# Where weight splits, two weight sums and a group of operand loads stand in the instruction order of a transformer-like layer

## The chip, the cores and the metric

The kernel runs on one core of a Trainium2 chip. The metric is the device time of one execution in microseconds (us); less is better. The median of three runs of the kernel before is 2864.06 us (2863.84 to 2871.59).

## The reference

One layer over 2048 tokens of width 1024, all in float32:

```python
xn = rms_norm(x, mix_norm_g)
aq, ak, av, mq, mk, mv, mo, i, f, ga, gm = split(xn @ w_in)
att = chunk_band_attention(aq, ak, av, rel_bias)      # chunks of 64, own and 8 previous
mq, mk = silu(causal_conv(mq)), silu(causal_conv(mk))
hm = mlstm_chunkwise(mq, mk, mv, i + b_i, f + b_f)    # matrix memory, a recurrence over chunks
m = sigmoid(mo) * headwise_rms_norm(hm)
y = sigmoid(ga) * (att @ w_att_proj) + sigmoid(gm) * (m @ w_mlstm_proj)
x = x + y @ w_out
x = x + square(relu(rms_norm(x) @ w_up)) @ w_down
return rms_norm(x, final_norm_g)
```

## The kernel before, in words

**Precision.** Every large product is made of three matmuls. A float32 operand is split into a rounded high part and the rest: ScalarE casts the high part (L435 for weights, L1032 and L1034 for activations), VectorE subtracts it from the operand (L437, L1037, L1039). A product is high by high, high by low and low by high (`mm3`, L496 to L498, and inline in the quads at L579 and L607).

**Weights.** A weight tile is 128 by 1024. It is loaded into one of four raw buffers (`wraw`) and split into one of three buffers (`wsplit`, two parts each); 459 tiles are split in this way, in the order in which `weights` lists them. `split_w` loads a tile and splits it; `quad_w` does so for the seven tiles of a quad out of four loaded ones. A raw buffer goes back to its pool with `late=LATE`, 3000 ns, and a split buffer goes back without, when the last matmul that reads it has been issued (the `fl.put(self.wsplit, w)` in `feature_tile`, `token_tiles`, `pair_tile`, `quad`, `quad_tok` and `down`).

**Quads.** Large products are computed on blocks of two by two with seven products in place of eight (Strassen's scheme in Winograd's form). A quad is seven weight tiles, m = 0 to 6, each multiplied with one of seven operands, and needs sums of weight blocks: `sum_w(q)` computes four of them for weight q, in two halves. For each half it takes four `ctx` tiles at once, loads four blocks (L399), does four subtractions on VectorE (L404) and stores their results to the DRAM tensor `wsum` (L1937); the second subtraction waits for the first store. The loader waits for these sums before it loads them (L417). Where the sums are made as the quad runs, `quad_w` does it on the raw tiles (L454). A quad's products share three PSUM places; `combine` adds them up with ScalarE copies (L1678) and VectorE adds (L1686), and a place is filled again only after its copy or add.

**Order.** Each engine runs its instructions in the order in which the program issues them. This order is written by a planner, `Flow`: each piece of work is a Python generator that yields waits, requests for buffers, and steps on an engine with an estimated length. The planner always issues the step that can start first by its own clock; among equal ones it goes by a priority, in which 0 (the splits) is before 1 (evacuations), 2 and 3 (the sums). `put(pool, item, late=...)` gives a buffer back at the planner's present time plus `late`; whoever takes it can't start before that by the planner's clock. `late` puts no wait into the program; it only moves the taker's instructions back in the order. Real waits are the semaphores between engines, which follow from the data and the buffers.

**Stages** (`dense`, priority 5, issues the main matmuls). The sequence has four blocks of 512 tokens. Block 0 and block 1 have their own input projections; beside them run the attention (L1196, L1227, L1258, L1263, L1208) and the recurrence (L1483 to L1556) of the block before. Then come, as pairs of weights, the projections of block 0 (`proj`); the quads of the gates ga0, ga1, gm0, gm1 for blocks 0 and 1; the projection of block 1 and the two quads of `w_out`; eleven quads of `w_in` for blocks 2 and 3, two of which (`quad_tok`, L607, for the values) have fourteen tiles with twelve matmuls each, where the others have 24 matmuls a tile; eight quads of `w_up` and the products with `w_down`; and the same from the projections on for blocks 2 and 3, whose attention and recurrence run beside the first `w_down`.

**The two sums.** Weights q = 2 and 3 are the quads of `w_out`. Their `sum_w` is spawned at the end of block 0's input projections, so it runs beside block 1. The other sums are spawned at the beginning of quads of `w_in` and `w_up`.

**The stored projection and the output operands.** `project_span(s)` projects block 2s+1 with `project`, whose results stay in eight `ctx` tiles (`y3`, set at L864 together with the event `yp_ev[2s+1]`). `take_rest`, one for each k from 0 to 3, takes three more `ctx` tiles, loads two tiles of the other block's projection into them (L1603), and makes from them and two of the eight kept ones the operands 2 to 6 of the w_out quad (adds at L1616, splits at L1034 and L1039). `load` in `after_out` takes eight `ctx` tiles, one after the other, and loads the residual input x into them (L1885), from the middle of the projection on (the event `go`). The quad's products are added to these (L1898). The pool `ctx` has sixteen tiles.

Of the kernel before, what the change touches and what calls it, by code (L numbers as in the profile page):

```python
# [45 lines left out]
N_G, N_O, N_F = 2, 2, 8  # L46
# [4 lines left out]
GATES = ("ga0", "ga1", "gm0", "gm1")  # L51
# [171 lines left out]


class Layer:
    LATE = 3000.0

    def __init__(self, tc, pool, psum, io):
        self.tc, self.nc, self.io = tc, tc.nc, io
# [95 lines left out]
    def weights(self):  # L325
# [12 lines left out]
        for name in GATES:  # L338
            yield quad(name)
# [75 lines left out]
    def split_w(self, i, src, raw, sent=None):  # L415
# [4 lines left out]
        yield from self.split_now(i, raw)  # L420
        self.fl.put(self.wraw, raw, late=self.LATE)

# [18 lines left out]
    def quad_w(self, i, q, kept, raws, evs):  # L441
# [33 lines left out]
        yield from sub(2, b, d, b)  # L475
        fl.put(self.wraw, d, late=self.LATE)
        yield "wait", [spilt[1]]
        yield from sub(3, a, c, a)
        fl.put(self.wraw, c, late=self.LATE)
        yield from self.split_now(i + 5, b)  # L480
        yield "wait", [spilt[2]]
        fl.put(self.wraw, b, late=self.LATE)
        yield from self.split_now(i + 6, a)
        yield "wait", [spilt[3]]
        fl.put(self.wraw, a, late=self.LATE)

# [13 lines left out]
    def feature_tile(self, srcs, evs, parts=1):  # L500

        fl = self.fl
        w = yield from self.next_w()
        wv = w.rearrange("p a (k c) -> p a k c", k=KT)
        got = []
        n = KT // parts
        for k in range(KT):
            if k % n == 0:
                got += (yield "dense", self.banks, 1)
            if evs[k] is not None:  # L510
                yield "wait", [evs[k]]
            yield "pe", 681
            self.mm3(got[-1], wv[:, 0, k], wv[:, 1, k], srcs[k][:, 0], srcs[k][:, 1],
                     k % n == 0, k % n == n - 1)
        fl.put(self.wsplit, w)
        return got

    def token_tiles(self, srcs, evs, after):

        fl = self.fl  # L520
        bank = [None] * NT
        nw = len(srcs) // 2
        for i in range(nw):
            w = yield from self.next_w()
            wv = w.rearrange("p a (k c) -> p a k c", k=2)
            for t in range(NT):
                if i == 0:
                    (bank[t],) = yield "dense", self.banks, 1
                for k in range(2):
                    g = 2 * i + k  # L530
                    if evs[g] is not None:
                        yield "wait", [evs[g]]
                    yield "pe", 681
                    a = srcs[g][:, :, t * P:(t + 1) * P]
                    self.mm3(bank[t], a[:, 0], a[:, 1], wv[:, 0, k], wv[:, 1, k],
                             g == 0, g == 2 * nw - 1)
                if i == nw - 1:
                    fl.spawn(after(t, bank[t]), 1)
            fl.put(self.wsplit, w)

    def pair_tile(self, srcs, evs, kind="dense"):

        fl = self.fl
        w = yield from self.next_w()
        wv = w.rearrange("p a (k n c) -> p a k n c", k=4, n=2)
        got = []
        for n in range(2):
            got += (yield kind, self.banks, 1)
            for k in range(4):
                if evs[k] is not None:  # L550
                    yield "wait", [evs[k]]
                yield "pe", 681
                self.mm3(got[-1], wv[:, 0, k, n], wv[:, 1, k, n], srcs[k][:, 0], srcs[k][:, 1], k == 0, k == 3)
        fl.put(self.wsplit, w)
        return got

    def quad(self, A, aev, after, release):


        fl = self.fl  # L560
        bank, clear = {}, {}
        mm = self.nc.tensor.matmul
        for m, z in enumerate(PLACES):
            w = yield from self.next_w()
            wv = w.rearrange("p a (k n c) -> p a k n c", k=4, n=2)
            for n in range(2):
                new = (z, n) not in bank
                if new:
                    (bank[z, n],) = yield "get", self.banks, 1
                else:  # L570
                    yield "wait", [clear[z, n]]
                ps = bank[z, n]
                for k in range(4):
                    if aev[m][k] is not None:
                        yield "wait", [aev[m][k]]
                    yield "pe", 681
                    a = A[m][k]
                    for x, y in ((0, 0), (0, 1), (1, 0)):
                        mm(ps, wv[:, x, k, n], a[:, y], start=new and k == 0 and x == y == 0,  # L579
                           stop=k == 3 and x == 1, skip_group_check=True)  # L580
                clear[z, n] = after(m, n, ps)
            fl.put(self.wsplit, w)
            if release:
                fl.put(self.rpool, *A[m])

    def quad_tok(self, p, A, aev, after):

        fl = self.fl
        bank, clear = {}, {}
        mm = self.nc.tensor.matmul  # L590
        for m, z in enumerate(PLACES):
            for kk in range(2):
                w = yield from self.next_w()
                wv = w.rearrange("p a (k c) -> p a k c", k=2)
                for n in range(2):
                    new = kk == 0 and (z, n) not in bank
                    if new:
                        (bank[z, n],) = yield "get", self.banks, 1
                    elif kk == 0:
                        yield "wait", [clear[z, n]]  # L600
                    ps = bank[z, n]
                    for k in range(2):
                        yield "wait", [aev[m][2 * kk + k]]
                        yield "pe", 681
                        a = A[m][2 * kk + k][:, :, (2 * p + n) * P:(2 * p + n + 1) * P]
                        for x, y in ((0, 0), (1, 0), (0, 1)):
                            mm(ps, a[:, y], wv[:, x, k], start=new and k == 0 and x == y == 0,  # L607
                               stop=kk == k == 1 and y == 1, skip_group_check=True)
                fl.put(self.wsplit, w)
            for n in range(2):  # L610
                clear[z, n] = after(m, n, bank[z, n])

    def down(self, s, m, ring, A, aev):

        fl = self.fl
        mm = self.nc.tensor.matmul
        bank = {}
        for c in range(4):
            for q in range(2):
                w = yield from self.next_w()  # L620
                wv = w.rearrange("p a (k n c) -> p a k n c", k=4, n=2)
                for n in range(2):
                    j = 2 * q + n
                    if c == 0:
                        (bank[j],) = yield "dense", self.banks, 1
                    for k in range(4):
                        yield "wait", [aev[m, c][k]]
                        yield "pe", 681
                        a = A[m, c, k]
                        self.mm3(bank[j], wv[:, 0, k, n], wv[:, 1, k, n], a[:, 0], a[:, 1],  # L630
                                 c == 0 and k == 0, c == 3 and k == 3)
                    if c == 3:
                        fl.spawn(self.add_down(s, m, j, bank[j]), 1)
                fl.put(self.wsplit, w)
            fl.put(ring, *[A[m, c, k] for k in range(4)])

    def dense(self):
        fl = self.fl
        none = [None] * KT
        for b in range(2):  # L640
# [40 lines left out]
                fl.spawn(self.evac_og(b, j, bk), 1)  # L681
            fl.put(self.rpool, *xs)
            fl.set(B["xs_free"])
            for q in range(N_G, N_G + N_O if b == 0 else 0):
                fl.spawn(self.sum_w(q), 3)
        for k in range(4):
            fl.spawn(self.take_rest(k, *G, self.xnd[:2], self.xn_kept[:2], 1.0), 2)

# [7 lines left out]
        fl.put(self.rpool, *self.blk[0]["mix"])  # L696
        self.banks.want = 0
        X, U = self.operands(), self.operands()
        for name in GATES:
            last = name == GATES[-1]  # L700
            if last:
                fl.spawn(self.take_mix(1), 1)
            yield from self.quad(*G, self.after_in(name, 0), release=last)
# [1161 lines left out]
    def after_out(self, s, q, U, go=None):  # L1865

        fl, nc = self.fl, self.nc
# [8 lines left out]
        def load():  # L1876
            if go is not None:
                yield "wait", [go]
            for w in ("a11", "a22", "a12", "a21"):
                for n in range(2):  # L1880
                    hi, h = where[w]
                    (x,) = yield "get", self.ctx, 1
                    xt[n][w] = x
                    yield "sp", 900, 2000
                    nc.sync.dma_start(x[:, :512], self.io["xt"][2 * s + h, 4 * hi + 2 * q + n])  # L1885
                    fl.set(ev[n][w])
# [454 lines left out]
```

## Time and profile before

| | us |
|---|---|
| median of three runs | 2864.06 |
| profiled execution | 2863.24 |
| its span | 2861.4 |
| TensorE matmuls busy | 2802.6 |
| VectorE busy | 2016.3 |
| ScalarE busy | 1529.6 |

Mean granted TensorE clock over the span is 0.997 of full speed. PE is TensorE, DVE VectorE, ACT ScalarE, SP or SPq SyncE, whose queue issues all the DMAs of data. A row of the groups reads: line, engine, operation, output and inputs, count, busy time and mean ns of one, and the idle time of the engine in front of it with what ended it. A row of the waits reads: who waited for whom, us in total, times, and the longest. In the order of time a row reads: start, duration, engine, line, operation, and in brackets the idle time before it and its releaser. Times of rows are counted from the span's start.

### The profile page before, as it was taken

The numbers are of one execution on the slowest core, as the hardware profiler recorded it, in microseconds if no ns is written. First come the engines' busy times: TensorE is split into PE (matmuls) and PEld (weight loads), VectorE is DVE, ScalarE is ACT, GpSimd is POOL, SyncE is SP. The second block draws the span as 40 slices with busy tenths as digits, with TensorE's granted clock in tenths as the row PEclk, the third lists the DMA queues.
The fourth block names the chain that finished last, engine by engine and source line by source line (L and its number), as shares of the span: only waits on it lengthen the run. The fifth ranks groups of instructions, "written<-read, shape, count | busy, mean of one in ns | idle before, by whom it ended". The sixth has DMA issues, their size and how long they took to land.

```text
span 2861.4 us, 39400 instructions
## 1 busy us (share of the span) xinstructions
PE 2802.6 (98%) x13528; PEld 2337.2 (82%) x13528; DVE 2016.3 (70%) x3745; ACT 1529.6 (53%) x2639; POOL 48.1 (2%) x100
## 2 busy tenths in 40 slices
PE   8999999999999999999999999999999999999998
PEld 7887888888878887878887888888887888888887
DVE  6795698657896866886667778789568744455565
ACT  5563467544354544575556566665435655554444
POOL 0010001000000000000000000000000000000000
PEclk9999999999999999999999999999999999999999
DMA  7878867648755687588877987876587655576563
GB/s 261 270 222 282 251 187 235 219 143 295 231 200 200 208 271 241 193 273 307 282 271 253 285 235 221 254 218 218 196 306 238 210 199 195 187 243 213 185 225 135
DMA packets 317736, 662.41 MB, mean 231 GB/s; under 512 B 35552, under 2 KB 62304, under 8 KB 317536
## 3 DMA queue, kind: packets, MB, share of 16 engines
q1 hardware_dynamic: 317536, 659.90, 70.3%
q8 instruction: 106, 1.74, 0.3%
q14 instruction: 94, 0.77, 0.1%
HBM read 462.63 MB, written 197.13 MB: 231 GB/s over the span
## 4 chain that ended last, share of the span: by engine, by line
PE 72%; DVE 13%; DMA 9%; ACT 3%; issue 2%; SPq 1%; POOL 0%; POOLq 0%; DVEq 0%; ACTq 0%
PE bank L579 32%; PE bank L496 10%; PE bank L497 10%; PE bank L498 10%; DVE wsp L437 3%; PE bank L607 2%; PE bank L1196 2%; DMA wsum<-ctx 2%; DVE r L1037 2%; DMA r<-u 1%; PE bank L1258 1%; PE bank L1227 1%; ACT wsp L435 1%; DVE sc L1233 1%; DMA ctx<-in_wf 1%
## 5 line engine op out<-in xcount | busy, mean ns | idle before, releaser
L579 PE MATMUL bank<-r,wsp 128*128 128x512 f32 x5544 | 1266.4, 390 | 11.7 <-DVE ctx L1686 6.7
L579 PEld LDWEIGHTS bank<-r,wsp 128*128 128x128 f32 x5544 | 1038.2, 188 | 232.9 <-DVE ctx L1686 8.9
L437 DVE TENSOR_TENSOR wsp<-wraw,wsp 128x1024 fp32r<-128x1024 f32 x459 | 560.4, 1221 | 366.2 <-ACT wsp L435 346.5
L435 ACT CAST wsp<-wraw 128x1024 fp32r<-128x1024 f32 x459 | 481.7, 1050 | 499.4 <-PE bank L579 210.5
L496 PE MATMUL bank<-r,wsp 128*128 128x512 f32 x1472 | 588.8, 400 | 3.0 <-DVE tmp L1208 1.8
L498 PE MATMUL bank<-r,wsp 128*128 128x512 f32 x1472 | 575.4, 391 | 0.0
L497 PE MATMUL bank<-r,wsp 128*128 128x512 f32 x1472 | 575.1, 391 | 0.0
L498 PEld LDWEIGHTS bank<-r,wsp 128*128 128x128 f32 x1472 | 276.5, 188 | 59.4
L496 PEld LDWEIGHTS bank<-r,wsp 128*128 128x128 f32 x1472 | 277.0, 188 | 52.2 <-DVE tmp L1208 2.7
L497 PEld LDWEIGHTS bank<-r,wsp 128*128 128x128 f32 x1472 | 277.2, 188 | 47.6
L1032 ACT CAST r<-r 128x512 fp32r<-128x512 f32 x264 | 161.0, 622 | 85.7 <-DMA r<-u 66.8
L1037 DVE TENSOR_TENSOR r<-r 128x512 fp32r<-128x512 f32 x264 | 175.8, 686 | 35.0 <-ACT r L1032 33.5
L1686 DVE TENSOR_TENSOR ctx<-bank,ctx 128x512 f32<-128x512 f32 x186 | 126.8, 686 | 84.8 <-PE bank L579 83.8
L1242 ACT ACTIVATE sc<-sc,scs 128x640 f32<-128x640 f32 (+4 forms) x128 | 97.7, 764 | 94.7 <-DVE scs L1239 88.0
L1678 ACT COPY ctx<-bank 128x512 f32<-128x512 f32 x186 | 108.0, 582 | 71.0 <-PE bank L579 65.2
L404 DVE TENSOR_TENSOR ctx<-ctx,ctx 128x512 f32<-128x512 f32 x112 | 76.6, 690 | 61.4 <-DMA ctx<-in_wf 40.8
L2014 ACT ACTIVATE ctx<-ctx 128x512 f32<-128x512 f32 x96 | 60.6, 632 | 107.0 <-DVE ctx L1686 107.0
L1233 DVE CUSTOM_DVE_ANT_0 sc<-bank,bias 128x320 f32<-128x320 f32 (+3 forms) x240 | 105.4, 459 | 12.7 <-PE bank L1227 10.7
L1196 PE MATMUL bank<-r,r 128*128 128x256 f32 (+1 forms) x672 | 108.7, 283 | 5.3 <-DVE r L1263 4.4
L1196 PEld LDWEIGHTS bank<-r,r 128*128 128x128 f32 x672 | 98.5, 191 | 17.3 <-DVE r L1263 7.8
L1263 DVE TENSOR_TENSOR r<-bank,r 128x512 fp32r<-128x512 f32 (+1 forms) x168 | 96.0, 593 | 14.4 <-ACT r L1261 13.5
L454 DVE TENSOR_TENSOR wraw<-wraw,wraw 128x1024 f32<-128x1024 f32 x76 | 92.6, 1219 | 5.3 <-DMA wraw<-in_wf 3.7
(247 smaller groups left out, 2781.4 us busy)
## 6 DMA issues: line engine op xcount, KB each, us to landing
wraw<-in_wf SPq DMA_DIRECT2D x178, 512.0 KB, 4.2
wraw<-wsum SPq DMA_DIRECT2D x136, 512.0 KB, 3.8
r<-u SPq DMA_DIRECT2D x224, 256.0 KB, 4.1
wraw<-in_w SPq DMA_DIRECT2D x88, 512.0 KB, 4.4
u<-ctx SPq DMA_DIRECT2D x128, 256.0 KB, 2.7
ctx<-in_wf SPq DMA_DIRECT2D x112, 256.0 KB, 3.9
wsum<-ctx SPq DMA_DIRECT2D x112, 256.0 KB, 4.0
u<-tmp SPq DMA_DIRECT2D x96, 256.0 KB, 3.2
```

What stands on the lines that cost most here:

```text
L435: nc.scalar.copy(w[:, 0], raw)
L437: nc.vector.tensor_sub(w[:, 1], raw, w[:, 0].bitcast(F32))
L496: mm(ps, lh, rh, start=first, stop=False)
L497: mm(ps, lh, rl, start=False, stop=False)
L498: mm(ps, ll, rh, start=False, stop=last)
L579: mm(ps, wv[:, x, k, n], a[:, y], start=new and k == 0 and x == y == 0, stop=k == 3 and x == 1, skip_group_check=True)
L1032: self.nc.scalar.copy(dst[:, 0], src)
L1037: self.nc.vector.tensor_sub(dst[:, 1], src, dst[:, 0].bitcast(F32))
L1196: nc.tensor.matmul(bk[:, c0:c0 + w], st, sl[:, x, o:o + w], start=n == 0, stop=n == total - 1)
L1233: nc.vector.tensor_tensor_reduce(out=e[:, x * w:x * w + w], in0=bks[x][:, :w], in1=br[:, j0 + x * w:j0 + x * w + w], op0=ALU.add, op1=ALU. ...
L1678: nc.scalar.copy(t[:, o:o + 512], ps)
L1686: nc.vector.tensor_add(t[:, o:o + 512], ps, t[:, o:o + 512])
```

## The change

Three edits. A split buffer goes back with `late=2500` ns at its six places. The two `sum_w` of the w_out weights are spawned at the beginning of the quads ga1 and gm0 in place of the end of block 0. In `load`, for the first w_out quad of a span, the third to eighth operand are taken and loaded after all eight events of the stored projection.

```diff
-    LATE = 3000.0
+    LATE, LATE_SPLIT = 3000.0, 2500.0
...
-        fl.put(self.wsplit, w)
+        fl.put(self.wsplit, w, late=self.LATE_SPLIT)
...
             fl.set(B["xs_free"])
-            for q in range(N_G, N_G + N_O if b == 0 else 0):
-                fl.spawn(self.sum_w(q), 3)
...
-        for name in GATES:
+        for i, name in enumerate(GATES):
             last = name == GATES[-1]
+            if 0 < i < 3:
+                fl.spawn(self.sum_w(N_G + i - 1), 3)
...
             for w in ("a11", "a22", "a12", "a21"):
                 for n in range(2):
                     hi, h = where[w]
+                    if go is not None and w == "a22" and n == 0:
+                        yield "wait", self.yp_ev[2 * s + 1]
                     (x,) = yield "get", self.ctx, 1
```

The second hunk stands for all six places (`feature_tile`, `token_tiles`, `pair_tile`, `quad`, `quad_tok`, `down`). No matmul, cast, subtraction or DMA is added or left out.

More of the change, by code (lines that the diff above doesn't have):

```diff
@@ L538, in token_tiles @@
                     fl.spawn(after(t, bank[t]), 1)
-            fl.put(self.wsplit, w)
+            fl.put(self.wsplit, w, late=self.LATE_SPLIT)
     def pair_tile(self, srcs, evs, kind="dense"):
@@ L553, in pair_tile @@
                 self.mm3(got[-1], wv[:, 0, k, n], wv[:, 1, k, n], srcs[k][:, 0], srcs[k][:, 1], k == 0, k == 3)
-        fl.put(self.wsplit, w)
+        fl.put(self.wsplit, w, late=self.LATE_SPLIT)
         return got
@@ L581, in quad @@
                 clear[z, n] = after(m, n, ps)
-            fl.put(self.wsplit, w)
+            fl.put(self.wsplit, w, late=self.LATE_SPLIT)
             if release:
@@ L608, in quad_tok @@
                                stop=kk == k == 1 and y == 1, skip_group_check=True)
-                fl.put(self.wsplit, w)
+                fl.put(self.wsplit, w, late=self.LATE_SPLIT)
             for n in range(2):
@@ L633, in down @@
                         fl.spawn(self.add_down(s, m, j, bank[j]), 1)
-                fl.put(self.wsplit, w)
+                fl.put(self.wsplit, w, late=self.LATE_SPLIT)
             fl.put(ring, *[A[m, c, k] for k in range(4)])
```

## The prediction

> **What bounds the kernel now.** I read the page's busy times first, then the list of what TensorE (PE) waits for, then the instructions in order of time around its long waits.
>
> ```profile
> span 2861.4 us, 39400 instructions
> PE 2802.6 (98%) x13528; PEld 2337.2 (82%) x13528; DVE 2016.3 (70%) x3745; ACT 1529.6 (53%) x2639; POOL 48.1 (2%) x100
> ...
> L437 DVE TENSOR_TENSOR wsp<-wraw,wsp 128x1024 fp32r<-128x1024 f32 x459 | 560.4, 1221 | 366.2 <-ACT wsp L435 346.5
> L435 ACT CAST wsp<-wraw 128x1024 fp32r<-128x1024 f32 x459 | 481.7, 1050 | 499.4 <-PE bank L579 210.5
> ```
>
> PE is busy for 2802.6 of 2861.4 us, and the change neither adds nor removes a matmul. So a gain can only come out of the 58.8 us in which PE stands idle, and out of slow clock. The waits of PE by what ended them:
>
> ```profile
> PE bank L496 <- ACT wsp L435: 7.5, 1, 7.5
> PE bank L579 <- DVE ctx L1686: 6.7, 7, 1.8
> PE bank L1521 <- DVE cst L1524: 4.7, 4, 2.2
> PE bank L1196 <- DVE r L1263: 4.4, 9, 1.2
> PE bank L1519 <- DVE ctx L1507: 3.6, 2, 3.4
> PE bank L579 <- ACT r L1034: 3.0, 2, 1.5
> PE bank L607 <- DVE ctx L1686: 2.6, 2, 2.2
> PE bank L1258 <- DVE tmp L1208: 2.4, 3, 1.2
> ...
> PE bank L579 <- DVE ctx L1898: 1.3, 1, 1.3
> ```
>
> The columns are us in total, times, longest. The first row is the start, which stays. L1686 (9.3 us over two rows) is the add that clears a PSUM bank in the quads; L1034 and L1898 belong to the quads of w_out; L1507, L1524, L1263 and L1208 are the recurrence and the attention. Each of the three edits aims at one of these groups.
>
> **The two sums.** They leave block 1 and go beside the quads ga1 and gm0. This is where they stand now; columns are start, duration, engine, line, and in brackets the idle time before:
>
> ```profile
> 228.36 1.14 ACT L1487 ACTIVATE ctx<-bank,g_u 128x128 f32<-128x128 f32 x4 [4.11 <-issue]
> ...
> 228.66 0.69 DVE L404 TENSOR_TENSOR ctx<-ctx,ctx 128x512 f32<-128x512 f32 x1 [3.22 <-DMA wsum<-ctx]
> 229.27 1.22 DVE L437 TENSOR_TENSOR wsp<-wraw,wsp 128x1024 fp32r<-128x1024 f32 x1
> 230.41 1.28 DVE L404 TENSOR_TENSOR ctx<-ctx,ctx 128x512 f32<-128x512 f32 x2
> 231.61 0.68 DVE L1507 SCALAR_TENSOR_TENSOR ctx<-bank,ctx 128x512 f32<-128x512 f32 x1
> ...
> 232.35 0.80 PE L1519 MATMUL bank<-r,ctx 128*128 128x129 f32 x2 [3.39 <-DVE ctx L1507]
> ```
>
> VectorE stood 3.22 us in front of a subtraction (L404) that waits for its own store to `wsum`. Behind it came a split and two more subtractions, and only then L1507, for which PE waited 3.39 us. Without the sums L1507 still needs ScalarE's four exponentials, which end at 228.36 + 1.14 = 229.50; with its own 0.68 it ends near 230.2, so that PE, idle since 232.35 - 3.39 = 228.96, waits about 1.3 us. That saves 2.1 us. The stall has a second price, the clock (columns: window, length, then busy time with counts for PE, weight load, DVE, ACT, POOL, then PE clock, DMA share, GB/s):
>
> ```profile
> 233.00:239.00 6.00, 6.00 (x25) 5.17 (x25) 1.87 (x3) 2.18 (x5) 0.00 (x0) 0.59 1.04 337
> 484.00:488.00 4.00, 4.00 (x18) 3.67 (x18) 2.97 (x7) 3.46 (x10) 0.00 (x0) 0.62 0.65 214
> 540.00:690.00 150.00, 149.11 (x658) 123.11 (x658) 88.82 (x105) 70.73 (x106) 1.01 (x1) 1.00 0.61 203
> ```
>
> After the stall six microseconds ran at 0.59: 6 x 0.41 = 2.4 us lost. Together 4.5 us, at most 3.4 + 2.4 = 5.8, at least nothing, if other work of block 1 fills the same places.
>
> What the move costs is read from the place it goes to: in 540 to 690 us PE is busy 149.11 of 150, VectorE 59%, the DMA engines 61%. The two sums bring 2 x 2 halves x 4 = 16 subtractions, 16 x 0.69 = 11 us of the 61 that VectorE has free there, and 16 loads and 16 stores on SyncE's queue (8.4 MB, 56 GB/s more over 150 us). Whether a waiting L404 holds up a bank-clearing add is seen where such sums already stand beside quads:
>
> ```profile
> L404 DVE TENSOR_TENSOR ctx<-ctx,ctx 128x512 f32<-128x512 f32 x112 | 76.6, 690 | 61.4 <-DMA ctx<-in_wf 40.8
> ...
> PE bank L579 <- DVE ctx L1686: 5.8, 6, 1.8
> ...
> 711.66 0.32 SPq L417 DMA_DIRECT2D wraw<-wsum  x1
> ```
>
> In 540 to 1550 us, where twelve of the fourteen sums (112 / 8) run, the quads waited 5.8 us for L1686. If all of that is put down to sums, one costs 0.5 us, two cost 1.0; bounds 0 and 3.6 (two of the longest wait, 1.8). The next in line, the first load of the two `wsum`s, is issued at 711.66 today, and the sums start when ga1 and gm0 begin, near 572 and 610 us; a half takes some 15 us in the rows above, so they end with 50 us to spare. Net: -4.5 + 1.0 = **-3.5 us** (from -5.8 to +3.6).
>
> **The output operands.** `load` now takes two `ctx` tiles, and the other six only when the eight tiles of the stored projection are there. Today:
>
> ```profile
> 721.20 0.33 SPq L1885 DMA_DIRECT2D ctx<-in_xt  x1
> ...
> 745.79 0.33 SPq L1603 DMA_DIRECT2D ctx<-yp  x1
> ...
> 749.89 0.73 PE L579 MATMUL bank<-r,wsp 128*128 128x512 f32 x2 [1.47 <-ACT r L1034]
> ...
> 2159.85 0.32 SPq L1603 DMA_DIRECT2D ctx<-yp  x1
> ...
> 2157.32 6.89 PE L579 MATMUL bank<-r,wsp 128*128 128x512 f32 x29 [1.29 <-DVE ctx L1898]
> 2165.73 0.73 PE L579 MATMUL bank<-r,wsp 128*128 128x512 f32 x2 [1.52 <-ACT r L1034]
> 2166.88 3.48 PE L579 MATMUL bank<-r,wsp 128*128 128x512 f32 x14 [0.41 <-DVE r L1039]
> ```
>
> L1885 is the load of these operands, L1603 that of `take_rest`, which needs three `ctx` tiles per k and makes the quad's third to seventh operands. Its last load goes out 25 us after the operand loads (745.79), and at 2159.85 in the second span, when tiles come free; PE then waits for its split (L1034). The pool has 16 tiles; eight hold the projection's sums and up to eight the operands, so the last `take_rest` finds none. With two in place of eight there is room for two `take_rest` at a time. At stake is 1.47 + 1.29 + 1.52 + 0.41 = 4.7 us. What is late next is the a22 operand itself: its load (4.1 us median from issue to landing, next row) must be back when the quad's third product is done, some 16 us after the quad began.
>
> ```profile
> DMA to landing us min/median/max: 2.6/4.1/6.3
> ```
>
> I take 3.5 of the 4.7: **-3.5 us**; bounds -4.7, and +4 if the load is one landing late once.
>
> The page "Perfetto Trace Analysis" of the Trainium skill (section "Optimization Strategy") has repeated bubbles as a sign that buffers ran out; these four rows look like that, and by it all 4.7 us would go.
>
> **The splits.** 459 weight tiles are split by one cast (1050 ns) and one subtraction (1221 ns). With the buffer counted as free 2.5 us later, the pair is put behind whatever ScalarE and VectorE start in those 2.5 us. ScalarE stands idle 499.4 us before these casts, and in order, so work behind them waits too. The raw tile's reload on SyncE is listed 3 us behind the split, before and after, and moves along; four raw tiles give it more room than the three split ones. One case, at 1126 us:
>
> ```profile
> 1123.59 1.98 ACT L435 CAST wsp<-wraw 128x1024 fp32r<-128x1024 f32 x2
> ...
> 1124.65 1.23 DVE L437 TENSOR_TENSOR wsp<-wraw,wsp 128x1024 fp32r<-128x1024 f32 x1 [0.79 <-ACT wsp L435]
> 1125.79 1.28 DVE L1686 TENSOR_TENSOR ctx<-bank,ctx 128x512 f32<-128x512 f32 x2
> ...
> 1126.62 0.70 PE L607 MATMUL bank<-wsp,r 128*128 128x512 f32 x2 [2.19 <-DVE ctx L1686]
> ```
>
> Two adds that free PE's bank stood behind a split that nobody was in haste for. Of the 9.3 us of such waits I take a third, -3. In attention and recurrence (L1524, L1263, L1208: 11.5 us) VectorE is nearly full and the split, listed later, still takes 1.22 us of it; a quarter, -3.
>
> Against this stands the place where a tile lasts shortest, the two quads of the values:
>
> ```profile
> 976.33 33.03 PE L607 MATMUL bank<-wsp,r 128*128 128x512 f32 x144
> ...
> 1001.23 1.05 ACT L435 CAST wsp<-wraw 128x1024 fp32r<-128x1024 f32 x1 [1.07 <-PE bank L607]
> ...
> 1002.90 1.22 DVE L437 TENSOR_TENSOR wsp<-wraw,wsp 128x1024 fp32r<-128x1024 f32 x1
> ```
>
> Twelve matmuls a tile make 33.03 / 12 = 2.75 us, and with three buffers a split has 2 x 2.75 = 5.5 us from release to use. The cast at 1001.23 started at the release; the split ended at 1004.12, 2.9 us later. That leaves 2.6 us, and 2.5 are given away. 28 tiles are in these two quads; at 0.15 us of wait for each, +4. Elsewhere a tile has 24 matmuls and twice the room. Net **-2 us**; bounds -15 (two thirds of 9.3 and all but a few us of the rest) and +20 (0.9 us on each of 28, less a part of the gains).
>
> **Sum.** -3.5 - 3.5 - 2 = -9. The profiled execution took 2863.24 us (its span and 1.8 us around it), 0.8 below the median of 2864.06. So 2854.2 on its scale, **2855 us** beside the median.
>
> **Rivals.** (1) *Weights come late in the value quads.* From 2.6 us of delay after a release PE waits; a split that is listed the full 2.5 us later has no room for even one add of 0.68 us ahead of its subtraction. At 0.9 us for each of 28 tiles it is 25 us in place of 4: 2855 + 21 = 2876, slower. The same page and section of the skill has one make a dependency that holds an engine start sooner, and this edit does the opposite; by that rule this rival is the outcome. For it: the 2.6 against 2.5. Against it: the queues run on as soon as they can, so few splits are really 2.5 us late. 13%.
> (2) *Waits only move.* VectorE stays as loaded, the quads' and the attention's waits come back elsewhere, or the later mark alters little, since 366 us of VectorE's idle time is before splits as it is; what stays is half of the first two edits, -3.5: 2860. 27%.
> (3) *The splits were what held the adds.* Two thirds of 9.3 and half of 11.5 go, -12, value quads at +2: with the first two -17, 2847. 18%.
> The forecast itself, 2849 to 2861, has 42%.
>
> On the clock, the page "TensorE: Matmul & The Clock Gate" (section "HAM oscillation — how this bites in real kernels") warns of idle gaps of over some 3.4 us. The row 484 to 488 shows 0.62 after a wait of only 2.2 us (the longest for L1524), so the trace is stricter; by the rule a new stall of 2.5 us would cost just itself, by the trace 4 x 0.38 = 1.5 us more.
>
> **How the numbers follow.** A measurement of this kernel tells about 0.3% from none, 8.6 us, so faster is below 2855.5 and slower above 2872.7. The forecast gives 0.28 faster and 0.14 same, rival 3 0.18 faster, rival 2 0.05 faster and 0.22 same, rival 1 0.13 slower: 0.51, 0.36, 0.13. The range runs from 2842 (rival 3 and a little more) to 2871 (rival 1 with 0.75 us a tile); it takes in the bounds of the first two edits.
>
> **What would show it.** Sums: no PE wait for L1507 over 2 us near 230, clock 1.00 in 233 to 239, and less than 1.5 us of new PE idle time in 540 to 690. Operands: the L1603 loads before the last L1885, and the waits for L1034 gone from both spans. Splits: ScalarE's idle time before L435 well under 499 us, waits for L1686 under 7 us, and PE waits for L437 or L435 in the value quads of no more than 4 us in all. Wrong is the forecast if PE waits there by 0.5 us a tile, or if block 1 has new waits as long as the old.

## The result, and the profile after

The changed kernel takes 2856.95 us (median of seven runs, 2851.83 to 2862.11), the kernel before 2865.13 in the same comparison (2861.38 to 2871.59). The ratio is 0.9967, with a 95% interval of 0.9954 to 0.9981: 0.33% faster, 8.2 us between the medians. Predicted were 2855 us and a range of 2842 to 2871. The profiled execution took 2858.04 us.

From the page of the changed kernel, and below it the rows that matter here of what TensorE waits for (us in total, times, longest):

```profile
span 2856.3 us, 39412 instructions
PE 2801.4 (98%) x13528; PEld 2334.4 (82%) x13528; DVE 2014.5 (71%) x3743; ACT 1526.5 (53%) x2641; POOL 48.7 (2%) x100
...
L437 DVE TENSOR_TENSOR wsp<-wraw,wsp 128x1024 fp32r<-128x1024 f32 x459 | 560.9, 1222 | 345.6 <-ACT wsp L435 332.7
L435 ACT CAST wsp<-wraw 128x1024 fp32r<-128x1024 f32 x459 | 482.0, 1050 | 463.4 <-PE bank L579 195.6
```

```profile
PE bank L579 <- DVE ctx L1686: 13.5, 11, 3.0
PE bank L496 <- ACT wsp L435: 7.5, 1, 7.5
PE bank L1519 <- ACT wsp L435: 5.5, 2, 4.4
PE bank L1196 <- DVE r L1263: 3.3, 5, 1.0
...
PE bank L579 <- DVE ctx L1900: 2.8, 1, 2.8
PE bank L607 <- DVE ctx L1686: 2.4, 2, 2.0
...
PE bank L1258 <- DVE tmp L1208: 1.2, 2, 0.7
PE bank L579 <- ACT r L1034: 1.2, 1, 1.2
...
PE bank L1519 <- DVE ctx L1507: 0.4, 2, 0.2
```

TensorE's work is unchanged (2801.4 us busy against 2802.6), so the gain did come out of waits, but not out of those that were forecast. The wait at 232 us and those for L1524 have gone, those for L1034 have fallen from 3.0 to 1.2 us. The wait for L1898, which is L1900 in this kernel, has grown from 1.3 to 2.8 us and now stands in the second w_out quad of the second span. The waits for the adds in the quads (L1686), of which a third was to go, have grown from 9.3 to 13.5 + 2.4 = 15.9 us. And there is a new wait of 4.4 us, of the recurrence's matmul L1519 at 472 us. Its row names a weight cast (L435), but that had ended at 471.01 and the matmul began at 471.85: what ended just before it, at 471.74, is again L1507, whose result it reads. Three windows of the changed kernel, in the columns of the prediction's windows, show where the moved sums were, the new wait, and where the sums went:

```profile
229.00:235.00 6.00, 6.00 (x38) 5.28 (x37) 2.18 (x3) 2.41 (x6) 0.28 (x2) 1.00 0.96 275
472.00:478.00 6.00, 6.00 (x24) 5.58 (x25) 4.23 (x10) 3.50 (x11) 0.00 (x0) 0.53 0.96 334
540.00:690.00 150.00, 146.51 (x643) 120.05 (x642) 96.04 (x120) 68.15 (x100) 1.01 (x1) 1.00 0.74 245
```

Near 232 us there is no stall and full clock. At 472 us the clock is 0.53; at 233 us it was 0.59 before. Beside the gates' quads TensorE now idles for 3.5 us where it idled for 0.9, with 7 us more of work on VectorE (96.0 against 88.8) and 42 GB/s more on the DMA engines.

### The profile page after: what moved, and what is told of

Same layout as the page of the kernel before. It is cut to its first block, busy times and chain, and to the rows that moved or that the text cites. A ratio compares the mean times of both kernels' runs of the same rounds, so it can differ in the third digit from the quotient of the medians.

```text
span 2856.3 us, 39412 instructions
## 1 busy us (share of the span) xinstructions
PE 2801.4 (98%) x13528; PEld 2334.4 (82%) x13528; DVE 2014.5 (71%) x3743; ACT 1526.5 (53%) x2641; POOL 48.7 (2%) x100
## 4 chain that ended last, share of the span: by engine, by line
PE 72%; DVE 11%; DMA 10%; ACT 3%; issue 3%; SPq 1%; POOL 0%; POOLq 0%; DVEq 0%; ACTq 0%
PE bank L579 31%; PE bank L496 11%; PE bank L497 10%; PE bank L498 10%; DVE wsp L437 2%; PE bank L607 2%; DMA wsum<-ctx 2%; PE bank L1196 2%; PE bank L1227 2%; PE bank L1258 1%; DMA ctx<-in_wf 1%; ACT wsp L435 1%; DVE r L1037 1%; DVE ctx L1857 1%; DVE ctx L1686 1%
## 5 line engine op out<-in xcount | busy, mean ns | idle before, releaser
L579 PE MATMUL bank<-r,wsp 128*128 128x512 f32 x5544 | 1268.4, 390 | 17.5 <-DVE ctx L1686 13.5
L435 ACT CAST wsp<-wraw 128x1024 fp32r<-128x1024 f32 x459 | 482.0, 1050 | 463.4 <-PE bank L579 195.6
L1037 DVE TENSOR_TENSOR r<-r 128x512 fp32r<-128x512 f32 x264 | 176.5, 687 | 50.1 <-ACT r L1032 49.2
L1032 ACT CAST r<-r 128x512 fp32r<-128x512 f32 x264 | 160.0, 624 | 84.1 <-DMA r<-u 60.4
L1686 DVE TENSOR_TENSOR ctx<-bank,ctx 128x512 f32<-128x512 f32 x186 | 127.0, 687 | 78.9 <-PE bank L579 78.8
L404 DVE TENSOR_TENSOR ctx<-ctx,ctx 128x512 f32<-128x512 f32 x112 | 76.7, 689 | 72.5 <-DMA ctx<-in_wf 40.9
L1263 DVE TENSOR_TENSOR r<-bank,r 128x512 fp32r<-128x512 f32 (+1 forms) x168 | 96.3, 594 | 13.0 <-ACT r L1261 12.1
```

Source lines behind the costliest of these rows:

```text
L435: nc.scalar.copy(w[:, 0], raw)
L1032: self.nc.scalar.copy(dst[:, 0], src)
L1037: self.nc.vector.tensor_sub(dst[:, 1], src, dst[:, 0].bitcast(F32))
L1686: nc.vector.tensor_add(t[:, o:o + 512], ps, t[:, o:o + 512])
```

## The experiments

All ratios are against the kernel before, run on the same chip beside them (medians 2866.17, 2866.24 and 2866.48 us in the three groups); "us" for a ratio is its distance from 1 times that median.

**The three parts alone, and two together.** Each edit of the change was put into the kernel before by itself; the fourth run has the second and the third.

```diff
# e1: splits alone
-        fl.put(self.wsplit, w)
+        fl.put(self.wsplit, w, late=self.LATE_SPLIT)
# e2: sums alone
-            for q in range(N_G, N_G + N_O if b == 0 else 0):
-                fl.spawn(self.sum_w(q), 3)
...
+            if 0 < i < 3:
+                fl.spawn(self.sum_w(N_G + i - 1), 3)
# e3: operands alone
+                    if go is not None and w == "a22" and n == 0:
+                        yield "wait", self.yp_ev[2 * s + 1]
```

> The kernel before with the later mark on the split buffers alone (2500 ns at all six places). Forecast's theory: -2 us (ratio 0.999), waits of TensorE for the quads' adds (L1686) fall from 9.3 to about 6 us, with up to 4 us of new waits in the value quads. Rival, formed from the trace of the changed kernel, where the waits for L1686 have grown to 15.9 us: the later mark doesn't shorten these waits; they are 9 us or more here too, no waits for weights in the value quads, and the time is within 4 us of before either way. Second rival: the mark carries the gain, -6 us or more.

Measured: 2859.95 us, ratio 0.9979 (0.9966 to 0.9992), -6 us. The waits of TensorE in this run:

```profile
PE bank L579 <- DVE ctx L1686: 8.5, 8, 2.4
...
PE bank L607 <- DVE ctx L1686: 1.4, 2, 1.0
...
PE bank L607 <- DVE wsp L437: 0.4, 1, 0.4
```

Together 9.9 us for L1686, where 9.3 were before: the waits that the mark was to shorten have not fallen. In the stretch of the value quads the only wait for a split is one of 0.4 us. So the edit gains, more than forecast, and not in the way forecast. The first rival has the waits right, but 6 us is more than its "within 4 us" (the interval reaches from -9.7 to -2.3 us); the second has the size. In this run the waits at which the other two edits aim are nearly gone as well: 1.1 us are left of the 3.4 before L1519 in the middle of block 1, and 0.2 of the 4.7 in the first w_out quads. Others stand in their place, one of 3.2 us at 478 us among them. What the 6 us are made of can't be read from this trace: its execution took 2862.23 us, 1 us less than the profiled one of the kernel before.

> The kernel before with the two sums moved beside ga1 and gm0 alone. Forecast's theory: -3.5 us; the 3.4 us wait for L1507 near 232 us and the half clock behind it are gone, 1 us comes back in 540 to 690 us. Rival: block 1 gains more, 8 us or over, and the gates' quads take 3 us or more, together -5. Second rival: another long wait takes the place in block 1 (the changed kernel has one of 4.4 us near 472 us) with its half clock, and the net is within 2 us of nothing.

Measured: 2869.11 us, ratio 1.0006 (0.9993 to 1.0018): no gain. TensorE's waits of this run, the first two rows between 205 and 530 us, the last between 540 and 690 us:

```profile
PE bank L1258 <- DVE ctx L1556: 4.5, 1, 4.5
PE bank L1519 <- DVE ctx L1507: 2.5, 1, 2.5
...
PE bank L579 <- DVE ctx L1686: 5.0, 2, 2.5
```

the two long ones in the order of time, with L1507 near 232 us ahead of them:

```profile
226.07 0.69 DVE L1507 SCALAR_TENSOR_TENSOR ctx<-bank,ctx 128x512 f32<-128x512 f32 x1 [0.83 <-PE bank L1505]
...
456.41 1.18 PE L1258 MATMUL bank<-const,sc 128*128 128x128 f32 x6 [4.46 <-DVE ctx L1556]
...
478.36 0.49 PE L1519 MATMUL bank<-r,ctx 128*128 128x129 f32 x2 [2.45 <-DVE ctx L1507]
```

and the clock behind the first of them and at 233 us:

```profile
456.00:460.00 4.00, 3.59 (x13) 3.01 (x14) 4.00 (x15) 2.42 (x7) 0.00 (x0) 0.60 0.66 207
233.00:239.00 6.00, 6.00 (x40) 5.38 (x39) 2.81 (x11) 2.48 (x11) 0.00 (x0) 1.00 0.50 157
```

Near 232 us L1507 now runs at 226.07, as soon as its own matmuls (L1505) are done; TensorE has no wait there, and the clock is full (1.00 in 233 to 239). The 2.5 us for L1507 are another wait, at 478 us. But towards the end of block 1 there is one of 4.5 us, with a clock of 0.60 behind it, and the gates' quads wait 5.0 us where 0.9 were before. The second rival is what happened. The profiled execution was the slowest of the twelve (2876.87 us), so its waits together are more than those of the median. The long wait is no accident of it: all six profiled kernels with moved sums (this one, e4, e8, e9, e10 and the changed kernel) have one of 3.5 to 4.6 us between 450 and 475 us. In the eight with the sums in block 1 the longest wait between 440 and 530 us is 2.1 to 3.6 us; in the kernel before it is 2.2, at 483.

> The kernel before with the operand loads behind the stored projection alone. Forecast's theory: -3.5 us, with the waits for L1034, L1898 and L1039 in the two first quads of w_out down from 4.7 to about 1 us; everything ahead of the first projection span stays instruction by instruction as before. Rival: the wait only moves into the next quad (the changed kernel has 3.0 us in the second w_out quad of blocks 2 and 3), so 0 to -1 us.

Measured: 2859.95 us, ratio 0.998 (0.9968 to 0.9991), -5.7 us. The two first quads of w_out in this run have, in order of the two spans, no wait at all, and

```profile
PE bank L579 <- ACT r L1034: 1.4, 2, 1.0
```

against 1.47 and 3.22 us before. The queue of SyncE in the second span shows why: the last load of `take_rest` (L1603) has moved ahead of all but one of the operand loads, which are L1887 in this kernel.

```profile
2114.01 1.48 SPq L1887 DMA_DIRECT2D ctx<-in_xt  x1
...
2139.90 0.32 SPq L1603 DMA_DIRECT2D ctx<-yp  x1
2142.30 1.79 SPq L1887 DMA_DIRECT2D ctx<-in_xt  x2
```

It goes out 20 us earlier than before (2159.85), with the quad's beginning within 5 us of where it was. The forecast's theory holds; the rival's "0 to -1 us" lies outside the interval, and the next quad waits 0.4 us (L1900). The waits in these quads are down by 2.9 us, from 4.7 to 1.8; where the rest of the 5.7 comes from the trace doesn't show. No neighbour of this edit was run, but its effect on the order is local: up to 690 us the order of every engine is that of the kernel before, and of all VectorE's and ScalarE's instructions 95% and more stand at the same position in the order.

So this run is also a second execution of the same order up to 690 us. In it the two waits in block 1 with a slow clock behind them have full clock (the kernel before: 3.39 us at 232 us with 0.59, 2.20 us at 483 us with 0.62):

```profile
232.29 0.49 PE L1519 MATMUL bank<-r,ctx 128*128 128x129 f32 x2 [2.35 <-DVE ctx L1507]
...
480.61 0.49 PE L1521 MATMUL bank<-cst,r 128*128 128x129 f32 x2 [2.23 <-DVE cst L1524]
```

```profile
233.00:239.00 6.00, 6.00 (x38) 5.26 (x37) 2.33 (x5) 3.57 (x11) 0.00 (x0) 1.00 0.99 327
481.00:485.00 4.00, 4.00 (x26) 3.44 (x26) 3.77 (x10) 3.70 (x12) 0.00 (x0) 1.00 0.62 211
```

> The changed kernel without the later mark on the split buffers. Forecast's theory: -7 us against before, 2 us slower than the changed kernel. Rival (the mark brings nothing): as fast as the changed kernel, 0.9967 within 0.0015, or faster. Second rival (the mark carries the gain): -3 us or less.

Measured: 2861.34 us, ratio 0.9984 (0.9972 to 0.9996), -4.6 us. That is the operands' gain and nothing for the sums (0.998 x 1.0006 = 0.9986), and slower than the changed kernel's 0.9967, though the intervals overlap. Its interval (-8.0 to -1.1 us) takes in the forecast's -7 and the second rival's -3, so it doesn't choose between them. The parts multiply: 0.9979 x 1.0006 x 0.998 = 0.9965, where 0.9967 was measured.

**Without the moved sums.**

> The changed kernel with the two sums back beside block 1 (later mark and operand loads alone). Theory after the first four runs (the two gains add up, 0.9979 x 0.998, and the moved sums bring nothing or cost a little): ratio 0.996, about -11.5 us against before and 1 to 2 us faster than the changed kernel. Rival (the moved sums need the other two edits to pay): slower than the changed kernel, 0.998 or more.

```diff
# against the changed kernel
+            for q in range(N_G, N_G + N_O if b == 0 else 0):
+                fl.spawn(self.sum_w(q), 3)
...
-            if 0 < i < 3:
-                fl.spawn(self.sum_w(N_G + i - 1), 3)
```

Measured: 2856.95 us, ratio 0.9966 (0.9956 to 0.9976): the changed kernel's time to 0.01%. The whole gain is there without the second edit. That it would be faster than the changed kernel was not confirmed. The traces give a reason why moving the sums adds nothing to the later mark: with the sums still in block 1, the matmul that stood 3.39 us at 232 us in the kernel before stands 0.6 us here (1.1 in e1), with full clock in both.

```profile
236.16 0.46 PE L1519 MATMUL bank<-r,ctx 128*128 128x129 f32 x2 [0.62 <-issue]
```

**Where the later mark works.** The same edit in the two kinds of quads alone, and in the other four places alone.

```diff
# e6 in quad and quad_tok; e7 in feature_tile, token_tiles, pair_tile and down
-            fl.put(self.wsplit, w)
+            fl.put(self.wsplit, w, late=self.LATE_SPLIT)
```

> The kernel before with the later mark in the two kinds of quads alone (quad, quad_tok). Theory (the mark's gain comes from the quads, where splits stand ahead of the adds that free banks): -4 to -6 us. Rival (it comes from attention, recurrence and the down products): within 2 us of nothing. Second rival (weights late in the value quads): slower, with waits for L437 or L435 there.

> The kernel before with the later mark everywhere but in the quads (feature_tile, token_tiles, pair_tile, down). Theory (the gain comes from the quads): within 2 us of nothing. Rival (it comes from here): -4 to -6 us. Third possibility (any new order of the instructions shifts the time by some us, and no place carries it): the two halves don't add up to the -6 us of all six places.

Measured: 0.9988 (0.9976 to 1.0) in the quads, which is 3.4 us faster, and 1.0027 (1.0015 to 1.004) in the rest, which is 8 us slower. The product is 1.0015, where all six places together gave 0.9979. The halves don't add up, as the third possibility had it: what the mark does in one half depends on the other. Up to 620 us every engine has the same order in e7 as in e1, so the 14 us between these two arise behind that.

**The same mark, 0.1 us less.**

```diff
# against e1
-    LATE, LATE_SPLIT = 3000.0, 2500.0
+    LATE, LATE_SPLIT = 3000.0, 2400.0
```

> The kernel before with the later mark alone at all six places, at 2400 ns in place of 2500. Theory (the mark's gain is that of one order among many, since its two halves alone gave 0.9988 and 1.0027): the ratio differs from the 0.9979 of 2500 ns by 0.0015 or more, to either side, though no split is listed more than 0.1 us off. Rival (2.5 us of lateness is what gains): 0.998 again within 0.0013.

Measured: 2878.92 us, ratio 1.005 (1.0032 to 1.0069), 14 us slower than before and 20 us from the kernel with 2500 ns (1.005 - 0.9979 = 0.0071). Its waits are longer in many groups at once (the profiled execution was the slowest of the eight):

```profile
PE bank L579 <- DVE ctx L1686: 13.1, 7, 2.4
...
PE bank L1258 <- DVE tmp L1208: 6.0, 6, 2.4
PE bank L1196 <- DVE r L1263: 5.1, 7, 2.1
PE bank L1196 <- ACT r L1261: 4.3, 4, 2.2
```

No split is listed more than 0.1 us otherwise by the mark itself, but the planner picks whatever can start first, so one swapped pair changes what is picked behind it. The two orders part at 57 us on SyncE's queue, where a store and a load have changed places; first e1, then this run:

```profile
57.01 0.32 SPq L1937 DMA_DIRECT2D mvfar<-ctx  x1
57.42 0.84 SPq L417 DMA_DIRECT2D wraw<-in_w  x1
```

```profile
57.26 0.33 SPq L417 DMA_DIRECT2D wraw<-in_w  x1
57.77 0.79 SPq L1937 DMA_DIRECT2D mvfar<-ctx  x1
```

Of all VectorE's instructions 38% stand at the same position in both. 2500 ns is one order among many, and a good one.

**Loads listed as landing later.** Two of the planner's estimates were raised on the changed kernel: for the loads of all sums (e8), for those of the stored attention (e9), and both (e10); e11 is e10 with the sums beside block 1.

```diff
# e8, in sum_w
-                yield "sp", 900, 5000
+                yield "sp", 900, 10000
# e9, in take_mix and take_u1
-            fl.spawn(self.take_u1(self.mixd[b].ap()[i], r, B["mix_ev"][i]), 1)
+            fl.spawn(self.take_u1(self.mixd[b].ap()[i], r, B["mix_ev"][i], 5000), 1)
...
-    def take_u1(self, src, r, ev):
-        yield "sp", 900, 2000
+    def take_u1(self, src, r, ev, land=2000):
+        yield "sp", 900, land
```

> The changed kernel with the planner's estimate for the loads of all fourteen sums doubled from 5.0 to 10.0 us, so that their subtractions are listed some 5 us later behind their loads; no other edit. Theory (what the moved sums cost, and part of the waits for L1686 everywhere, is VectorE standing before subtractions whose loads haven't landed): VectorE's idle time before L404 falls from 72 us to under 30, TensorE's waits for L1686 from 15.9 us to 10 or less, and the time is 3 to 6 us below the changed kernel (0.995). Rival (those waits cover nothing that TensorE needs): no faster than the changed kernel.

Measured: 2853.1 us, ratio 0.996 (0.9944 to 0.9975). Its group of the sums' subtractions, and its waits of TensorE for L1686:

```profile
L404 DVE TENSOR_TENSOR ctx<-ctx,ctx 128x512 f32<-128x512 f32 x112 | 76.7, 689 | 68.9 <-DMA ctx<-in_wf 48.0
```

```profile
PE bank L579 <- DVE ctx L1686: 4.3, 4, 1.7
...
PE bank L607 <- DVE ctx L1686: 1.6, 2, 1.3
```

The waits for L1686 are down from 15.9 to 5.9 us, but VectorE's idle time before L404 isn't (68.9 against 72.5), so the mechanism that was expected did not do it. The interval includes the changed kernel's 0.9967: a gain over it isn't established.

> The changed kernel with one planner's estimate raised: the loads of the attention's stored results for a projection (take_mix) count as landing after 5.0 us in place of 2.0, so their splits (L1032) are listed some 3 us later. Theory (the 4.4 us wait near 472 us with 6.8 us of half clock behind it comes from ScalarE standing 3.4 us before L1032 whose load hasn't landed, with a weight split and the recurrence's exponentials behind it): that wait is gone or under 1.5 us, full clock there, 4 to 7 us faster than the changed kernel (0.9945). Rival (a long wait at the end of block 1 comes back at another instruction, as it has in every run with the moved sums): no faster than 0.9967 by more than 2 us.

Measured: 2859.64 us, ratio 0.998 (0.9966 to 0.9993), not faster. The wait is still there, because the order around it is still the same:

```profile
466.49 1.95 ACT L1032 CAST r<-r 128x512 fp32r<-128x512 f32 x3 [3.16 <-DMA r<-mix]
...
467.14 2.02 DVE L1037 TENSOR_TENSOR r<-r 128x512 fp32r<-128x512 f32 x3 [4.08 <-ACT r L1032]
469.19 0.69 DVE L1556 TENSOR_TENSOR ctx<-bank,r 128x512 f32<-128x512 f32 x1
470.31 0.72 DVE L1616 TENSOR_TENSOR ctx<-ctx,ctx 128x512 f32<-128x512 f32 x1 [0.43 <-DMA ctx<-xn]
470.95 0.68 DVE L1507 SCALAR_TENSOR_TENSOR ctx<-bank,ctx 128x512 f32<-128x512 f32 x1
...
471.73 0.46 PE L1519 MATMUL bank<-r,ctx 128*128 128x129 f32 x2 [4.42 <-ACT wsp L435]
```

The rows show ScalarE standing 3.16 us before L1032, whose load hadn't landed, and VectorE 4.08 us before L1037, which needs L1032's result; behind it come two more adds and only then L1507, which ends at 471.63, 0.1 us before L1519 begins. The weight cast that the last row names had ended at 470.90. So the theory has the late load right, but the way from it to TensorE leads over VectorE, not over the cast and the exponentials. The raised estimate didn't move L1032 and L1037 behind L1507, so the run doesn't decide whether this costs the 4.4 us.

> The two raised estimates together (sums' loads 10.0 us, stored attention 5.0 us) on the changed kernel. Theory: the gains of both add up, 0.993 to 0.994 against before. Rival: a long wait comes back elsewhere, 0.996.

> As the run before, but with the two sums back beside block 1. Theory (the place of the two sums doesn't matter once nothing stands in front of their loads): within 0.0015 of the run before. Rival (the moved sums pay once the wait at the end of block 1 is gone): slower than it by 4 us or more.

Measured: 0.9979 (0.9964 to 0.9995) and 0.999 (0.9974 to 1.0006). Neither raised estimate adds to the other, and with the sums in block 1 the time is within the stated 0.0015 of the run before. No version was found that is clearly faster than the changed kernel.

## Why the prediction was right or wrong

**The bound** held: TensorE's busy time stayed, and all that moved were waits and clock.

**The sums** (-3.5 us forecast) failed: alone they are at +1.7 us (-2.0 to +5.2), and taking them out of the change costs nothing. The step that failed is the net of what the move saves and costs. The wait at 232 us went as forecast, and wholly: the 1.3 us that were to stay rest on a misreading, since L1507 doesn't need the exponentials at 228.36 us, which are the next head's. In e2 it ran at 226.07, ahead of the same ones there (227.91). But the price of this wait was taken from one execution: in e3, with the same order, it is 2.35 us without a slow clock, where 4.5 us were reckoned as saved. Then "at least nothing, if other work of block 1 fills the same places" is what occurred, with a wait of 3.5 to 4.6 us towards the block's end. The cost beside the gates' quads, put at 1.0 us, was 4.1 more than before in e2 and 2.6 more in the changed kernel. And beside the later mark there was little left to save at 232 us. For this edit rival 2 was right.

**The output operands** (-3.5 us forecast) were right in mechanism: the loads change places as worked out and the waits of the first w_out quads go, to 1.8 us of 4.7 in e3 and 1.5 in e5, the second quad's included. In the changed kernel 4.0 us remain, 2.8 of them in the second quad, so there the rival of e3 has a part. The runs give -5.7 us (-9.2 to -2.6), which has 3.5 inside.

**The splits** (-2 us forecast) gain 6 us (2.3 to 9.7), and the terms are not the ones of the sum. "Of the 9.3 us of such waits I take a third" failed: 9.9 us remain with the mark alone, 15.9 with the whole change. Nor do these waits go with the time: they are 5.5 us in e7, whose profiled execution took 2864.47 us, and 15.9 in the changed kernel with 2858.04. Of the attention's and recurrence's waits (L1524, L1263 and L1208 in all rows, 13.9 us before) 12.5 us are left in e1, a tenth less and not a quarter. That the mark's size acts through lateness at all fell with 2400 ns, which is 20 us away. What stays open is which property of the order makes it fast; the runs show only that a small difference of it moves the time by more than the whole change.

**The value quads** (rival 1, +4 in the sum): not there. In the changed kernel the only waits of these quads are those for L1686 (2.4 us, against 2.6 before), none for a weight. "Against it: the queues run on as soon as they can" is borne out.

**The total** of -9 against the measured 8.2 between the medians is right with errors that cancel: some 5 us too much for the sums, some 2 and 4 too little for the operands and the splits. The range held, and so did the choice of side, on the operands' account by the reasons given, on the splits' by chance.

## What to carry to other kernels

Where a planner writes the order for queues that run in order, a planning number moves the time by changing the order everywhere; try its neighbours (2400 beside 2500) before giving a gain to what the number means, and test halves of the edit for whether they add up. A removed stall counts only when the next long wait behind it has been looked for: here the one at 232 us went, and each kernel with moved sums has one of 3.5 to 4.6 us at 456 or 472 us. And what a stall costs is not to be read from one execution: a second one of the same order had 2.35 us in place of 3.39, and full clock. Buffers that are taken long before they are used can be found in the profile as a load that goes out late although its data are there; moving the taker behind its competitor is an edit whose gain can be worked out from the rows.

## What the runs showed of the hardware that was not expected

The clock does not follow the length of a single wait. In the changed kernel a wait of 2.98 us is followed by a lower clock and one of 2.69 us is not, while before the change one of 2.20 us was (0.62 in 484 to 488 us). The same wait in e3, 2.23 us long, wasn't (1.00 in 481 to 485 us, shown there):

```profile
1240.51 1.84 PE L579 MATMUL bank<-r,wsp 128*128 128x512 f32 x7 [2.69 <-DVE ctx L1686]
...
1477.34 0.89 PE L579 MATMUL bank<-r,wsp 128*128 128x512 f32 x2 [2.98 <-DVE ctx L1686]
```

```profile
1240.00:1246.00 6.00, 5.33 (x22) 4.12 (x23) 4.72 (x7) 5.19 (x8) 0.00 (x0) 1.00 0.81 277
1477.00:1483.00 6.00, 5.66 (x18) 4.52 (x19) 3.80 (x5) 4.35 (x7) 0.00 (x0) 0.72 0.80 312
```

The first two are TensorE in order of time, the other two the windows behind these waits, all of the changed kernel; the last is TensorE before the change:

```profile
483.15 0.49 PE L1521 MATMUL bank<-cst,r 128*128 128x129 f32 x2 [2.20 <-DVE cst L1524]
```

And one program's executions differ by more than the change: the kernel before took between 2856.47 and 2878.03 us in 31 runs on one chip, so one profiled execution shows which waits there are, but its sum of waits is not that of the median.
